# A third buffer for the expert weights' chunks, their product moved later, and VectorE's background work cut smaller

## The chip, the cores and the metric

The kernel runs on one core of a Trainium2 chip, as one launch that covers the whole two-block network. The metric is the device time of one execution in microseconds. Matrix products run on TensorE (PE in the rows; its weight loads are PEld), elementwise work on VectorE (DVE), ScalarE (ACT) and GpSimd (POOL); SyncE (SP) issues most of the loads, ScalarE most of the stores, GpSimd the gathers.

## What is computed

A two-layer block (attention, pooling and convolution branches, then a mixture of 16384 rank-one experts with product keys) is followed by a two-layer conformer block. All is float32. The change touches the expert layer and the start of the next layer's convolution:

```python
def peer_ffn(x, w_q, sub_keys, u_emb, v_emb):          # per 128 tokens, 8 heads, 16 of 16384 experts each
    q = (xc @ w_q).reshape(PEER_CHUNK, PEER_HEADS, 2, PEER_HALF)
    s = jnp.einsum('thid,hikd->thik', q, sub_keys).astype(jnp.float32)
    s1, i1 = lax.top_k(s[:, :, 0], PEER_TOPK)
    s2, i2 = lax.top_k(s[:, :, 1], PEER_TOPK)
    cand = (s1[..., :, None] + s2[..., None, :]).reshape(PEER_CHUNK, PEER_HEADS, PEER_TOPK * PEER_TOPK)
    ...
    gate = jax.nn.softmax(top_s, axis=-1)
    hid = jax.nn.gelu(jnp.einsum('td,thkd->thk', xc, u_emb[eidx]))
    return jnp.einsum('thk,thkd->td', gate * hid, v_emb[eidx])
```

## The kernel before

Every float32 product is made of three matmuls on parts that are split: ScalarE copies a weight tile `raw` into `wh` (rounded to the type that TensorE takes), VectorE or, every few tiles, GpSimd subtracts and leaves `wl` (lines 212 and 223, class `Stream`). `Stream` loads the weight tiles in one fixed order through a ring of five `raw` buffers on SP's queue (line 200); `wl` has a ring of three. `W.pool_every` says which splits GpSimd takes.

The expert layer (`peer`) doesn't gather for its first 384 tokens in layer 0: it multiplies them by all 16384 experts. A **first loop** (128 steps, line 1634 on) makes 128 experts' activations a step from the tile `u`: 24 matmuls of 384 columns, a gelu on ScalarE into `gstage` (ring of three), and a store to `gel` every two steps. Beside it VectorE finds the top keys (`topk_keys`, `route`) and builds from them, with TensorE (line 1531), a dense matrix of gates that goes to `gmat` in twelve stores of 2048 KB. The **second loop** (128 steps, line 1697 on) multiplies by the tile `vv`. Its other operand comes in chunks of four steps: `wload` fetches `gelc` from `gel` and `gmc` from `gmat` (768 KB each) on SP's queue, `wmul` multiplies them on VectorE (line 1604), `wsplit` splits one step's row of the product into `Wh` and `Wl` (ring of four each), two steps ahead of the matmuls (line 1692, 18 of 512 columns a step). Chunks have a ring of two.

The other 128 tokens (`gat`) do gather: 256 times GpSimd fetches a row per token (512 KB in all, `gr`, ring of four, line 1399), and VectorE uses it (lines 1408 and 1423). These run beside both loops; what is left of them is spread over layer 1's convolution and gates (`tail`). Layer 1's modulation is computed by VectorE from raw tiles `modt` (line 516), also in the second loop.

What stands when in each queue is decided as the program is written: `Side` keeps a model of the engines' times. Background work is a generator (`topk_keys`, `route`, `gathered`); each `yield step(...)` is a place at which it may be put off, and `took(engine, ns)` books its cost. `tick` is called between matmuls and runs background steps while neither VectorE nor ScalarE is booked more than `LIM` = 2000 ns ahead. The instructions then stand in that order for good, and every engine works through its own queue in order.

Of the kernel before, what the change touches and what calls it, by code (L numbers as in the profile page):

```python
# [10 lines left out]
F32 = mybir.dt.float32  # L11
F32R = mybir.dt.float32r
# [257 lines left out]
class Side:  # L270
# [8 lines left out]
    def __init__(self, period, ring):  # L279
        self.lanes, self.lates = [], []  # L280
        self.period, self.ring = period, ring
        self.now = self.due = 0.0
        self.slot = [0.0] * 4
        self.free = {"a": 0.0, "v": 0.0, "p": 0.0}
        self.seq = 0
        self.floor = False
        self.rate, self.pe = RATE, 1.0

# [85 lines left out]
    def tick(self, dt):  # L374
        self.now += dt * self.pe
        while True:
            while any(x[0] <= self.now for x in self.lates):
                self._late()
            if self.now < self.due or max(self.free["v"], self.free["a"]) > self.now + LIM:
                return  # L380
            for lane in self.lanes:
                if self._ready(lane[1]) <= self.now:
                    self._run(lane)
                    break
            else:
                return
# [18 lines left out]
def tile_dit_peer_conformer(ctx: ExitStack, tc: tile.TileContext, A, out):  # L405
# [834 lines left out]
    def seg_tail(pool, ns, upd, halves, hs, ss, ab, banks, fill=None, then=None):  # L1240
# [9 lines left out]
        if fill is None:  # L1250
            norm_cols(pool, xs, ab[0], 0, 2 if ns == 2 else 3, banks, then)
            W.pool_every = 0 if ns == 1 else 2
            W.pump(3)
            if ns == 2:
                rest(2)
            return
# [13 lines left out]
    def peer(l, hcp, kp, keys, early):  # L1270
# [14 lines left out]
        with ExitStack() as st:  # L1285
# [37 lines left out]
            def took(eng, ns):  # L1323
                return cur["side"].spend(eng, ns) if sp and cur["side"] else 0.0
# [35 lines left out]
            if sp:  # L1360
                side.rate, side.pe = RATE2, 1.09
            sel = select()
# [65 lines left out]
            def route():  # L1428
                for t in (range(nt) if not sp else (3, 0, 1, 2)):
                    v4 = sv[:, t].rearrange("p (h i) k -> p h i k", i=2)  # L1430
                    cand = tk.tile([128, 8, 16, 16], F32, name="cand", bufs=1)
                    if sp:
                        yield step()
                    for h in range(8):
                        (nc.vector if sp else nc.gpsimd).tensor_add(cand[:, h], v4[:, h, 0, :, None].to_broadcast([128, 16, 16]),
                                                                    v4[:, h, 1, None, :].to_broadcast([128, 16, 16]))
                    took("v", 3000)
                    ts = tk.tile([128, 8, 16], F32, name="ts", bufs=2)
# [20 lines left out]
                    for i in range(2):  # L1459
                        for h0 in (0, 4):  # L1460
                            hh = slice(h0, h0 + 4)
                            eq = tk.tile([128, 4, 16, 16], F32, name="eq", bufs=1)
                            nc.vector.tensor_tensor(eq, abf[:, i, hh, :, None].to_broadcast([128, 4, 16, 16]),
                                                    iota16[:, None, None, :].to_broadcast([128, 4, 16, 16]), op=OP.is_equal)
                            nc.vector.tensor_mul(eq, eq, sif[:, hh, i, None, :].to_broadcast([128, 4, 16, 16]))
                            nc.vector.tensor_reduce(IN[:, t, i].rearrange("p (h k) -> p h k", h=8)[:, hh], eq, axis=AX.X, op=OP.add)
                            took("v", 3700)
                            yield step(TKW * 1.3)
# [86 lines left out]
                for q in range(0, TD // 4, 2):  # L1555
                    if sp:
# [4 lines left out]
                    nc.vector.tensor_tensor(Am, iotac[:, None, :].to_broadcast([128, 8, 128]),  # L1561
                                            IT[:, 1, q * 4:q * 4 + 8, None].to_broadcast([128, 8, 128]), op=OP.is_equal)
                    nc.vector.tensor_tensor(Bk, iotas, spread(IT[:, 0], q), op=OP.is_equal)
                    took("v", 1950)
                    if len(pend) > 2:
# [27 lines left out]
            def wload(c):  # L1593
                g = vq.tile([128, CI, TD], F32, name="gelc", bufs=2)
                nc.sync.dma_start(g, gel_d[c])
                m = vq.tile([128, ntb, CI, TB], F32, name="gmc", bufs=2)
                nc.sync.dma_start(m, g_d[:, :, c * CI:(c + 1) * CI, :].rearrange("b p c t -> p b c t"))
                ld[c] = (g, m)
# [12 lines left out]
            def wsplit(i):  # L1611
                c, r = divmod(i, CI)
                g = ld[c][0]
                wh = vp.tile([128, TD], F32R, name="Wh", bufs=4)
                wl = vp.tile([128, TD], F32R, name="Wl", bufs=4)
                split(wh, wl, g[:, r])
# [9 lines left out]
            for i in range(128):  # L1626
# [3 lines left out]
                if i % GB == 0:  # L1630
                    gs = gp.tile([128, GB, TD], F32, name="gstage", bufs=3)
                h, lo = W.next("u", l, i)
# [19 lines left out]
                if i == 118:  # L1652
# [8 lines left out]
                    vq = vq_stack.enter_context(tc.tile_pool(name=f"pw{l}", bufs=2))  # L1661
                    wload(0)
                    wload(1)
                    if l == 0:
# [32 lines left out]
            for i in range(128):  # L1697
                c, r = divmod(i, CI)
                if r == 0 and c + 1 < nch:
                    wmul(c + 1)  # L1700
                if i + 2 < 128:
                    wsplit(i + 2)
                if r == CI - 1 and c + 2 < nch:
                    wload(c + 2)
# [732 lines left out]
```

## Time and profile before

| | us |
|---|---|
| median of 3 runs | 4544.48 (4543.31 to 4550.07) |
| the profiled execution | 4539.79 |
| its span, first to last instruction | 4538.0 |
| layer 0's first expert loop | 816 to 1434 |
| layer 0's second expert loop | 1434 to 2215 |
| layer 1's convolution and gates with the last gathered rows | 2215 to 2400 |
| layer 1's second expert loop | 3142 to 3505 |

All times in the rows are from the span's start. The stages' bounds are where the rows of the lines named above begin and end. A group of instructions is told by its line, its engine and what it writes and reads (`wl<-raw,wh`).

### The profile page before, as it was taken

The numbers are of one execution on the slowest core, as the hardware profiler recorded it, in microseconds if no ns is written. First come the engines' busy times: TensorE is split into PE (matmuls) and PEld (weight loads), VectorE is DVE, ScalarE is ACT, GpSimd is POOL, SyncE is SP. The second block draws the span as 40 slices with busy tenths as digits, with TensorE's granted clock in tenths as the row PEclk, the third lists the DMA queues.
The fourth block names the chain that finished last, engine by engine and source line by source line (L and its number), as shares of the span: only waits on it lengthen the run. The fifth ranks groups of instructions, "written<-read, shape, count | busy, mean of one in ns | idle before, by whom it ended". The sixth has DMA issues, their size and how long they took to land. (4 is left out here: it accounts for less than half of the span.)

```text
span 4538.0 us, 66430 instructions
## 1 busy us (share of the span) xinstructions
PE 4215.3 (93%) x25423; PEld 3735.4 (82%) x25423; DVE 3221.3 (71%) x5177; ACT 1970.2 (43%) x2939; POOL 1128.6 (25%) x871
## 2 busy tenths in 40 slices
PE   8999999999998877777779989999999999999999
PEld 5887878999997666666678879999887998999988
DVE  6747766999996766566786878786666577555855
ACT  4224443334662222222334444575445445444544
POOL 0012343333117412222543446201443000000000
PEclk9999999999999888888899989999999999999999
DMA  6532232456889877878783336778886644556344
GB/s 218 166 99 69 72 101 97 151 194 234 293 293 343 278 259 270 289 276 283 249 301 110 107 124 206 237 282 306 281 280 237 215 154 132 187 181 215 116 160 156
DMA packets 304824, 932.29 MB, mean 205 GB/s; under 512 B 27752, under 2 KB 95736, under 8 KB 299640
## 3 DMA queue, kind: packets, MB, share of 16 engines
q1 hardware_dynamic: 244000, 696.86, 46.1%
q0 software_dynamic: 37040, 135.29, 8.3%
q10 hardware_dynamic: 23464, 95.88, 5.6%
q8 instruction: 199, 3.26, 0.3%
q14 instruction: 121, 0.99, 0.1%
HBM read 841.94 MB, written 85.99 MB: 204 GB/s over the span
## 5 line engine op out<-in xcount | busy, mean ns | idle before, releaser
L212 ACT ACTIVATE wh<-raw 128x1024 fp32r<-128x1024 f32 (+1 forms) x1086 | 1131.4, 1045 | 1093.4 <-DMA raw<-in_vv 516.4
L469 PE MATMUL pA<-xH,wl 128*128 128x256 f32 (+2 forms) x4600 | 1422.0, 309 | 57.3 <-DVE wl L223 46.1
L223 DVE TENSOR_TENSOR wl<-raw,wh 128x1024 fp32r<-128x1024 f32 (+2 forms) x956 | 1185.5, 1249 | 365.2 <-issue 185.5
L467 PE MATMUL pA<-xH,wh 128*128 128x256 f32 (+2 forms) x4600 | 1439.6, 313 | 1.7 <-ACT xH L472 1.3
L468 PE MATMUL pA<-xL,wh 128*128 128x256 f32 (+2 forms) x4600 | 1417.2, 308 | 0.5 <-DVE xL L473 0.3
L469 PEld LDWEIGHTS pA<-xH,wl 128*128 128x128 f32 x4600 | 876.1, 190 | 93.0 <-DVE wl L223 55.4
L467 PEld LDWEIGHTS pA<-xH,wh 128*128 128x128 f32 x4600 | 877.0, 191 | 34.8 <-issue 6.0
L468 PEld LDWEIGHTS pA<-xL,wh 128*128 128x128 f32 x4600 | 877.1, 191 | 26.6 <-DVE xL L473 1.1
L223 POOL TENSOR_TENSOR wl<-raw,wh 128x1024 fp32r<-128x1024 f32 (+1 forms) x130 | 322.8, 2484 | 731.8 <-PE pA L469 362.8
L1692 PE MATMUL pA<-wl,Wh 128*128 128x512 f32 x1024 | 349.9, 424 | 150.4 <-DVE wl L223 150.4
L1692 PEld LDWEIGHTS pA<-wl,Wh 128*128 128x128 f32 x1024 | 203.2, 202 | 211.1 <-DVE wl L223 163.9
L1692 PE MATMUL pA<-wh,Wl 128*128 128x512 f32 x1024 | 344.5, 419 | 1.7 <-DVE Wl L473 1.7
L1692 PE MATMUL pA<-wh,Wh 128*128 128x512 f32 x1024 | 335.3, 409 | 6.2 <-ACT Wh L472 6.2
L1399 POOL DMA_INDIRECT gr<-in_ur,gi x128 | 185.8, 1451 | 530.9 <-DVE gr L1408 498.8
L468 PE MATMUL pA<-wl,xH 128*128 128x256 f32 (+2 forms) x800 | 272.1, 340 | 10.2 <-POOL wl L223 6.2
L467 PE MATMUL pA<-wh,xH 128*128 128x256 f32 (+2 forms) x800 | 277.9, 347 | 1.8 <-ACT xH L472 1.8
L469 PE MATMUL pA<-wh,xL 128*128 128x256 f32 (+2 forms) x800 | 271.5, 339 | 1.1 <-DVE xL L473 1.1
L1399 POOL DMA_INDIRECT gr<-in_vr,gi x128 | 176.3, 1377 | 340.1 <-DVE gx L1423 297.7
L1609 POOL TENSOR_TENSOR gelc<-gelc,gmc 128x256 f32<-128x256 f32 x128 | 147.9, 1189 | 422.4 <-DMA gmc<-gmat 398.6
L1692 PEld LDWEIGHTS pA<-wh,Wl 128*128 128x128 f32 x1024 | 206.8, 202 | 54.5 <-DVE Wl L473 2.4
L1692 PEld LDWEIGHTS pA<-wh,Wh 128*128 128x128 f32 x1024 | 200.3, 196 | 56.2 <-ACT Wh L472 6.5
L458 POOL TENSOR_TENSOR segr<-segr,nhalf 128x1 f32<-128x1 f32 (+1 forms) x24 | 13.9, 579 | 886.3 <-DVE segr L547 886.3
(456 smaller groups left out, 6305.4 us busy)
## 6 DMA issues: line engine op xcount, KB each, us to landing
raw<-in_u SPq DMA_DIRECT2D x256, 512.0 KB
raw<-in_vv SPq DMA_DIRECT2D x256, 512.0 KB
raw<-in_modt SPq DMA_DIRECT2D x80, 512.0 KB
gmat<-gst ACTq DMA_DIRECT2D x20, 2048.0 KB
raw<-in_conv SPq DMA_DIRECT2D x48, 512.0 KB
raw<-in_gate SPq DMA_DIRECT2D x48, 512.0 KB
gel<-gstage ACTq DMA_DIRECT2D x64, 384.0 KB
gelc<-gel SPq DMA_DIRECT2D x32, 768.0 KB
```

The lines of the kernel that those rows point to most:

```text
L212: self.nc.scalar.activation(h[:, :w], t[:, :w], AF.Copy)
L223: e.tensor_sub(lo[:, :w], t[:, :w], h[:, :w].bitcast(F32))
L458: nc.gpsimd.tensor_tensor(r, r, nhalf[:, 0:1].to_broadcast([128, w]), op=OP.pow)
L467: nc.tensor.matmul(o, s[0], m[0], start=start, stop=False)
L468: nc.tensor.matmul(o, s[0], m[1], start=False, stop=False)
L469: nc.tensor.matmul(o, s[1], m[0], start=False, stop=stop)
L1399: nc.gpsimd.indirect_dma_start(t, None, tabs[j // 128], bass.IndirectOffsetOnAxis(ap=gi[:, k:k + 1], axis=0))
L1609: nc.gpsimd.tensor_mul(gv, gv, m[:, :, ci])
L1692: nc.tensor.matmul(acc[t][dh], s_, m_[:, dh * 512:(dh + 1) * 512], start=(i == 0 and n == 0), stop=(i == 127 and n == 2))
```

## The change

In layer 0 (`sp`): `gelc` and `gmc` get three buffers, three chunks are loaded ahead of the second loop, and chunk c+3 is asked for at the third step of chunk c. The product `wmul(c + 1)` moves from a chunk's first step to its third, next to the first split that reads it. `Wh` and `Wl` go from four buffers to three and `gstage` from three to two. For VectorE's background the limit is 1200 ns in place of 2000, the eight sums for `cand` are booked one by one with a place to put off after four, the three instructions of each `eq` chain get such places between them, and two bookings are adjusted. The tail of layer 0 leaves `W.pool_every` at 0, so GpSimd takes no split in layer 1's first conv tiles.

```diff
@@ class Side @@
-        self.rate, self.pe = RATE, 1.0
+        self.rate, self.pe, self.lim = RATE, 1.0, LIM
-            if self.now < self.due or max(self.free["v"], self.free["a"]) > self.now + LIM:
+            if self.now < self.due or self.free["v"] > self.now + self.lim or self.free["a"] > self.now + LIM:
@@ seg_tail @@
-            W.pool_every = 0 if ns == 1 else 2
+            W.pool_every = 0
@@ peer @@
-                side.rate, side.pe = RATE2, 1.09
+                side.rate, side.pe, side.lim = RATE2, 1.09, 1200
@@ route @@
                     for h in range(8):
+                        if sp and h == 4:
+                            yield step()
                         (nc.vector if sp else nc.gpsimd).tensor_add(cand[:, h], ...
-                    took("v", 3000)
+                        took("v", 380)
...
                             nc.vector.tensor_tensor(eq, abf[:, i, hh, :, None].to_broadcast([128, 4, 16, 16]),
+                            took("v", 1250)
+                            if sp:
+                                yield step()
                             nc.vector.tensor_mul(eq, eq, sif[:, hh, i, None, :].to_broadcast([128, 4, 16, 16]))
+                            took("v", 1250)
+                            if sp:
+                                yield step()
                             nc.vector.tensor_reduce(IN[:, t, i].rearrange("p (h k) -> p h k", h=8)[:, hh], eq, axis=AX.X, op=OP.add)
-                            took("v", 3700)
+                            took("v", 1250)
@@ wload, wsplit, the loops @@
-                g = vq.tile([128, CI, TD], F32, name="gelc", bufs=2)
+                g = vq.tile([128, CI, TD], F32, name="gelc", bufs=3 if sp else 2)
-                m = vq.tile([128, ntb, CI, TB], F32, name="gmc", bufs=2)
+                m = vq.tile([128, ntb, CI, TB], F32, name="gmc", bufs=3 if sp else 2)
-                wh = vp.tile([128, TD], F32R, name="Wh", bufs=4)
-                wl = vp.tile([128, TD], F32R, name="Wl", bufs=4)
+                wh = vp.tile([128, TD], F32R, name="Wh", bufs=3 if sp else 4)
+                wl = vp.tile([128, TD], F32R, name="Wl", bufs=3 if sp else 4)
-                    gs = gp.tile([128, GB, TD], F32, name="gstage", bufs=3)
+                    gs = gp.tile([128, GB, TD], F32, name="gstage", bufs=2 if sp else 3)
-                    wload(0)
-                    wload(1)
+                    for c in range(3 if sp else 2):
+                        wload(c)
-                if r == 0 and c + 1 < nch:
+                if r == (CI - 2 if sp else 0) and c + 1 < nch:
                     wmul(c + 1)
                 if i + 2 < 128:
                     wsplit(i + 2)
-                if r == CI - 1 and c + 2 < nch:
+                if sp and r == CI - 2 and c + 3 < nch:
+                    wload(c + 3)
+                if not sp and r == CI - 1 and c + 2 < nch:
                     wload(c + 2)
```

The first place is the second loop. SP's queue of loads around chunk 11, before (the numbers tell buffers apart; `raw_14392` and `raw_14420` are the tiles of two steps):

```order
L200 DMA raw_14392<-in_vv 128x1024
L200 DMA raw_14420<-in_vv 128x1024
L1595 DMA gelc_14447<-gel0_11_5869 128x1536
L1597 DMA gmc_14449<-gmat0_5890 128x12x128
L200 DMA raw_14455<-in_vv 128x1024
```

VectorE's queue around the product of the same chunk, before:

```order
L1604 TENSOR_TENSOR gelc_14447<-gelc_14447,gmc_14449 128x1536
L473 TENSOR_TENSOR Wl_14485<-gelc_14318,Wh_14484 128x384
L223 TENSOR_TENSOR wl_14492<-raw_14392,wh_14451 128x1024
L473 TENSOR_TENSOR Wl_14515<-gelc_14318,Wh_14514 128x384
L223 TENSOR_TENSOR wl_14520<-raw_14420,wh_14490 128x1024
L1408 SCALAR_TENSOR_TENSOR gr_14378,gz_5918<-gr_14378,gx_5917 128x1024
```

Before, the product stands ahead of the splits of two tiles that SP asks for ahead of the chunk.

SP's queue around chunk 11, now:

```order
L200 DMA raw_14228<-in_vv 128x1024
L1604 DMA gelc_14259<-gel0_11_5869 128x1536
L1606 DMA gmc_14261<-gmat0_5890 128x12x128
L200 DMA raw_14267<-in_vv 128x1024
L200 DMA raw_14296<-in_modt 128x1024
L200 DMA raw_14302<-in_vv 128x1024
L200 DMA raw_14330<-in_vv 128x1024
L200 DMA raw_14359<-in_modt 128x1024
L200 DMA raw_14365<-in_vv 128x1024
L1604 DMA gelc_14390<-gel0_12_5870 128x1536
L1606 DMA gmc_14392<-gmat0_5890 128x12x128
L200 DMA raw_14398<-in_vv 128x1024
```

VectorE's queue around its product, now:

```order
L223 TENSOR_TENSOR wl_14490<-raw_14398,wh_14460 128x1024
L1408 SCALAR_TENSOR_TENSOR gr_14288,gz_5918<-gr_14288,gx_5917 128x1024
L1408 SCALAR_TENSOR_TENSOR gr_14351,gz_5918<-gr_14351,gx_5917 128x1024
L516 SCALAR_TENSOR_TENSOR sjunk_5907,modc1_98<-raw_14359,S_5906 128x1024 x2
L522 TENSOR_TENSOR modc1_98<-modc1_98,pcol_88 128x16
L1613 TENSOR_TENSOR gelc_14259<-gelc_14259,gmc_14261 128x1536
L473 TENSOR_TENSOR Wl_14523<-gelc_14259,Wh_14522 128x384
```

Now seven raw tiles, the last of them `raw_14398`, are asked for after the chunk and used ahead of its product, and the product stands right before the first split that reads it.

The second place is GpSimd's queue at the start of layer 1's convolution, before (the first row's gathers are those of the second loop):

```order
L1399 DMA gr<-in_vr,gi 128x1024 x4
L223 TENSOR_TENSOR wl<-raw,wh 128x1024
L1399 DMA gr<-in_vr,gi 128x1024 x3
L223 TENSOR_TENSOR wl<-raw,wh 128x1024
L1399 DMA gr<-in_vr,gi 128x1024 x26
```

and now:

```order
L682 TENSOR_TENSOR hc_13072<-hc_13072,tmpo 128x512 x2
L720 MEMSET upad_17515 128x272
L720 MEMSET upad_17516 128x272
L1399 DMA gr<-in_vr,gi 128x1024 x48
```

Five splits (two of them in the rows) left GpSimd's queue for VectorE's, and 65 gathers are issued here where 52 were.

## Rows read from the trace of the kernel before

**Rows 1.** The page's first part: each engine's busy us, share of the span, instructions.

```profile
PE 4215.3 (93%) x25423; PEld 3735.4 (82%) x25423; DVE 3221.3 (71%) x5177; ACT 1970.2 (43%) x2939; POOL 1128.6 (25%) x871
```

**Rows 2.** Windows: us, busy PE PEld DVE ACT POOL, clock, DMA share, GB/s.

```profile
880.00:1060.00 180.00, 168.31 (x935) 165.56 (x933) 175.04 (x313) 66.82 (x87) 66.29 (x31) 0.98 0.52 184
1060.00:1360.00 300.00, 298.10 (x2185) 282.83 (x2185) 278.79 (x361) 194.19 (x220) 54.33 (x34) 0.99 0.81 289
1360.00:1434.00 74.00, 63.30 (x343) 61.07 (x343) 45.71 (x65) 23.36 (x34) 48.43 (x54) 0.95 0.99 371
1434.00:2215.00 781.00, 617.63 (x2355) 484.42 (x2353) 512.10 (x641) 199.07 (x279) 242.18 (x203) 0.87 0.79 275
2215.00:2400.00 185.00, 145.28 (x1054) 139.10 (x1055) 155.99 (x174) 61.17 (x90) 92.95 (x69) 0.90 0.77 269
...
3142.00:3505.00 363.00, 360.48 (x1555) 289.62 (x1553) 239.24 (x267) 177.29 (x263) 135.88 (x115) 1.00 0.78 271
```

**Rows 3.** Waits of VectorE and TensorE, 1434 to 2215: us, times, longest.

```profile
DVE gelc L1604 <- DMA gmc<-gmat: 243.9, 29, 10.4
...
PE pA L1692 <- DVE wl L223: 150.4, 31, 7.8
```

**Rows 4.** Timeline around one chunk: start, us, instruction, idle time before it.

```profile
1709.39 1.22 PE L1692 MATMUL pA<-wl,Wh 128*128 128x512 f32 x2 [3.57 <-DVE wl L223]
...
1711.26 1.05 PE L1692 MATMUL pA<-wh,Wh 128*128 128x512 f32 x2
1712.11 1.05 PE L1692 MATMUL pA<-wl,Wh 128*128 128x512 f32 x2
...
1715.65 0.63 PE L1692 MATMUL pA<-wh,Wh 128*128 128x512 f32 x2
1716.11 0.63 PE L1692 MATMUL pA<-wl,Wh 128*128 128x512 f32 x2
...
1716.89 0.44 SPq L1597 DMA_DIRECT2D gmc<-gmat  x1
...
1730.02 1.76 DVE L1604 TENSOR_TENSOR gelc<-gelc,gmc 128x1536 f32<-128x1536 f32 x1 [9.00 <-DMA gmc<-gmat]
```

**Rows 5.** Windows again, three short ones.

```profile
1370.00:1380.00 10.00, 9.46 (x54) 9.14 (x52) 4.44 (x7) 3.48 (x5) 2.34 (x3) 1.00 1.01 409
...
1709.00:1714.00 5.00, 4.61 (x11) 3.65 (x12) 5.00 (x8) 0.95 (x1) 1.68 (x1) 0.50 0.60 165
...
2300.00:2360.00 60.00, 46.94 (x348) 44.82 (x347) 53.88 (x65) 19.90 (x28) 32.36 (x29) 0.91 0.91 334
```

**Rows 6.** DMA's busy share in tenths, 40 slices of 1 us from 1710.

```profile
DMA  6976998998999999999940006916869889999999
```

**Rows 7.** DMA packets of the second loop, 1434 to 2215.

```profile
DMA packets 96852, 214.78 MB, mean 275 GB/s; under 512 B 6064, under 2 KB 52144, under 8 KB 96816
```

**Rows 8.** The page's DMA issues: count and KB each.

```profile
gmat<-gst ACTq DMA_DIRECT2D x20, 2048.0 KB
...
gel<-gstage ACTq DMA_DIRECT2D x64, 384.0 KB
```

**Rows 9.** Waits of the first loop, 816 to 1434.

```profile
ACT gstage L1642 <- PE pA L469: 179.6, 74, 7.4
...
DVE gr L1408 <- DMA gr<-in_ur,gi: 28.2, 14, 6.3
...
PE pA L469 <- DVE wl L223: 22.5, 11, 3.0
```

**Rows 10.** Layer 1's convolution, 2215 to 2400: groups of VectorE and GpSimd, one wait.

```profile
L1423 DVE SCALAR_TENSOR_TENSOR gx<-gr,gz,gx 128x1024 f32<-128x1024 f32 x56 | 76.1, 1359 | 12.8 <-DMA gr<-in_vr,gi 12.0
L223 DVE TENSOR_TENSOR wl<-raw,wh 128x1024 fp32r<-128x1024 f32 x36 | 47.9, 1333 | 0.0
...
L223 POOL TENSOR_TENSOR wl<-raw,wh 128x1024 fp32r<-128x1024 f32 x6 | 15.8, 2628 | 21.2 <-ACT wh L212 21.2
...
PE pA L469 <- POOL wl L223: 9.2, 3, 3.9
```

More of the change, by code (lines that the diff above doesn't have):

```diff
@@ L1562, in route @@
                                             IT[:, 1, q * 4:q * 4 + 8, None].to_broadcast([128, 8, 128]), op=OP.is_equal)
+                    took("v", 1250)
                     nc.vector.tensor_tensor(Bk, iotas, spread(IT[:, 0], q), op=OP.is_equal)
-                    took("v", 1950)
+                    took("v", 700)
                     if len(pend) > 2:
```

## The prediction

> **What bounds the kernel now.** I read the stages first [rows 2], because the shares of the whole span [rows 1] average over stages with different limits: TensorE is busy 93% of it, so a gain can come only from a stage where it is not. The profiled execution took 4539.79 us, its span 4538.0; the median of the timed runs is 4.7 us longer, and I add that at the end. In layer 0's second expert loop (1434 to 2215 us) TensorE is busy 617.63 of 781.00 us at a granted clock of 0.87. In layer 1's second loop, which has neither gathered rows nor the modulation's raw tiles, it is busy 360.48 of 363.00 at 1.00. The first loop of layer 0 loses some 12 us between 880 and 1060 and 11 us at its end. Layer 1's convolution (2215 to 2400) loses 40.
>
> Next the waits of the second loop [rows 3]: VectorE stands 243.9 us, 29 times, in front of the product gelc*gmc for the DMA of gmc. TensorE then waits 150.4 us, 31 times, for VectorE's weight split, which is queued behind that product. One chunk of four steps in time [rows 4]: SP issues the load of gmc at 1716.89; VectorE is through with all else 9.00 us before 1730.02, where the product starts, 13 us after the issue. TensorE waits 3.57 us in the chunk before and then runs pairs of matmuls at 0.85 us where undisturbed ones take 0.466; the clock's row for that place is 0.50 [rows 5], the lower of its two levels.
>
> Last the sixteen DMA engines (below: the link) in the same stretch [rows 6]: sixteen slices in a row at 0.8 and more, then one at 0.4 and three at nothing. The link is full while the late chunk is carried and idle while everybody catches up. Its mean share is 0.79 at 275 GB/s [rows 2], so the chunk's wait is only half latency: behind it stands a link that is not far from full.
>
> **Part 1: three chunk buffers, a late product.** On SP a chunk's loads now stand seven raw tiles ahead of the one whose split is next to the product; before, the product stood ahead even of a split whose tile had been asked for earlier than the chunk. Seven tiles are five steps and two of the modulation's: 30 us at the loop's pace of 781/128 = 6.1 us a step, and still 21 us at TensorE's best of 4.2 (below), against the 13 us of [rows 4]. So the wait for gmc goes. What is late next?
>
> TensorE alone: 128 steps x 18 matmuls x 0.233 us [rows 4] = 537 us. VectorE alone: 512 us busy [rows 2], less three gathered rows (counted on VectorE's order: 133 in this loop before, 130 now) = 508 us. The link: 214.78 MB were moved [rows 7], 212 without those rows (0.52 MB each) and without one chunk (1.57 MB) that is now loaded ahead. 275/0.79 = 348 GB/s is what a full link carries with this mix of packets (half of them under 2 KB), so 212 MB need 608 us. **The link is the longest, so the loop becomes link-bound**, at the share it can hold. Neighbouring stretches where much was queued hold 0.99 (1360 to 1434) and 0.91 (2300 to 2360) [rows 2, 5]; 0.89 is my lower end. That gives 614 to 683 us; I take 0.95, between the two rows since SP still issues in order behind VectorE's splits: 640 us, **141 us less** (98 to 167).
>
> Its costs. The third chunk is loaded before the loop, where the link is already full (0.99): 1.57 MB/0.371 = 4 us there, taken back in the loop (it is in the 212 MB). Wh and Wl with three buffers in place of four: the wl ring beside them has three already, and VectorE waits there for the same TensorE step as Wl would, so the wait moves half a microsecond forward: nothing. The gstage ring of two: a store must land in three steps and not five, and three steps are 3 x 618/128 = 14 us; it is 384 KB behind at most one store of 2048 KB [rows 8], 2.5 MB at 0.289 = 8.6 us. ScalarE's gelu waits 179.6 us for TensorE [rows 9], and no wait of it for a store is listed. Nothing, 12 times 1 us at worst.
>
> **Part 2: VectorE's background in smaller steps** (first loop). TensorE waits there 22.5 us for VectorE's splits [rows 9]. The work itself is unchanged and VectorE is 97% busy between 880 and 1060 (175.04 of 180), so smaller lumps only place it better. On the order the longest run of background between two splits falls by under 1 us (an eq chain of three instructions is cut only now and then). I take -4 us, from -15 to 0.
>
> **Part 3: gathered rows move back.** The tighter limit lets 10 fewer rows into the first loop (57, was 67), three fewer into the second, and 69 instead of 56 into layer 1's convolution and gates. There both are dense: VectorE 155.99 of 185, the link 0.77, and 0.91 in its middle [rows 2, 5]. By VectorE 13 rows cost 13 x 1.36 = 17.7 us [rows 10], by the link 13 x 0.52/0.334 = 20 us; idle time there (29 us of VectorE) may take up to half.
>
> **Part 4: no GpSimd splits in the first conv tiles.** Five splits of 2.63 us leave GpSimd and cost VectorE 5 x 1.33 = 6.7 us; TensorE's three waits for GpSimd's splits, 9.2 us, go [rows 10], and gathers are issued earlier. Parts 3 and 4 together: 10 + 6.7 to 20 + 6.7, less up to 9.2: +14 us, range +5 to +24.
>
> **The sum.** 4539.8 - 141 - 4 + 14 = 4409; with 4.7 for the median, **4413 us**. Its own range: 4539.8-167-15+5+4.7 = 4368 to 4539.8-98+24+4.7 = 4470.
>
> **The rivals.**
> (B) *The link gives more and TensorE bounds.* Between 1370 and 1380 us it carried 409 GB/s at 1.01 [rows 5]; 212 MB would need 518 us, under TensorE's 537. Then 537 + 10 for the start = 547: -234 - 4 + 14 gives 4320. Against it: that stretch holds large packets, while half of this loop's are under 2 KB [rows 7]. The Trainium skill (DMA: Bandwidth & Descriptors, Specifications) gives 435 GB/s as the fabric's ceiling and about 358 as a core's share of the HBM. By the first 212 MB would take 487 us, which is this rival; by the second 592, which is my forecast's side; the trace's 348 at a full link agrees with the second.
> (C) *Short waits remain and keep the clock low.* A link-bound loop still has a wait in most chunks, and after the wait in [rows 4] six pairs ran at 0.85 instead of 0.466, 2.5 us. Then a chunk costs 16.8 + 2.5 + the 2.2 us by which the link is late = 21.5 us, 32 of them 688: -93 - 4 + 18 gives 4465. For it: the clock is at 0.87 over this loop [rows 2]. Against: TensorE has 2.2 us a chunk to spare if waits are shorter than 3.57 us. The Trainium skill (TensorE: Matmul & The Clock Gate, HAM oscillation) says that a loop that waits for a DMA at every tile starts every tile at the low clock; this trace agrees for the waits of [rows 4], and shows 0.98 and 0.99 from 880 to 1360, where no wait is over 3.0 us [rows 2, 9].
> (D) *Slower: the wait changes its name.* With the link full, VectorE could wait for gathered rows or raw tiles as it now waits for gmc, for instance behind four gather buffers that are no deeper than before. If all 243.9 us come back, the loop stays at 781 and the convolution pays 13 rows and five splits in full: 20 + 6.7 gives 4571. It decides once the loop gains under 27 us, that is if the link's share stays below 608/754 = 0.81. For it: in the first loop VectorE waits 28.2 us for gathered rows [rows 9], with the link at 0.81 and, at its end, 0.99 [rows 2]. Against it: TensorE is busy 63.30 of 74.00 us in just that end, which is 0.86 and not the 0.79 of this loop.
> (E) *The chunk wait stays*, because SP's issue of the loads is itself held by a split: 4535 to 4553. Against it: the order has the loads seven tiles earlier.
>
> **How the numbers follow.** Forecast 0.60, C 0.20, B 0.12, D 0.05, E 0.03. The prediction is the forecast's 4413. The range 4350 to 4485 holds the forecast's own range and C with some room for it, and leaves out B, D and E (0.20). Within 0.2% (about 9 us, what a measurement of this kernel can tell from no change) lies E: 0.03; faster 0.92, slower 0.05.
>
> **What would show it.** In the second loop: VectorE's wait for gmc under 30 us; the link's share 0.92 or more; 615 to 680 us; ScalarE's wait for raw tiles (DMA) as what ends last. A share under 0.85 with waits for gathered rows speaks for D; a clock below 0.9 with a share near 0.88 for C; TensorE busy over 97% for B. In the first loop ScalarE's gelu must not wait for a DMA. In layer 1's convolution: 69 gathered rows, 5 to 24 us more, no split of GpSimd among TensorE's waits. It would be wrong altogether if the loop's bytes were not the 212 MB counted here, or if a full link carried this mix at another rate than 348 GB/s.

## The result and the profile after

The changed kernel takes 4361.73 us (median of 4 runs, 4359.04 to 4364.86) against 4543.9 beside it: ratio 0.9602, interval 0.9582 to 0.9622. In five more runs it took 4363.14, ratio 0.9612 (0.9599 to 0.9625). The forecast was 4413. The profiled execution took 4364.86 us. The page's first part, to be read against [rows 1]: TensorE's busy time has fallen by 56 us and the span by 175, so its share has risen.

```profile
PE 4158.8 (95%) x25423; PEld 3692.2 (85%) x25423; DVE 3223.1 (74%) x5180; ACT 1968.2 (45%) x2939; POOL 1123.1 (26%) x868
```

The stages are cut at two lines. The second loop of layer 0 runs from the first start of its matmuls (line 1692 before, 1701 after) to the last start of its `pB<-wl,Wh`; the convolution and gates of layer 1 end with the last start of L784. The view of one line of the kernel before (instructions, ns min/median/max, first and last start):

```profile
L1692 PE MATMUL pA<-wh,Wh x1024: 388/396/796, 1444.1 to 3501.6; 128*128 128x512 f32 x171
L1692 PE MATMUL pB<-wl,Wh x256: 389/396/632, 1452.1 to 2212.0; 128*128 128x512 f32 x128
...
L784 DVE SCALAR_TENSOR_TENSOR merged<-sig,pA x16: 409/548/689, 202.0 to 2391.6; 128x512 f32<-128x512 f32 x8, 128x256 f32<-128x256 f32 x8
```

and of the changed one:

```profile
L1701 PE MATMUL pA<-wh,Wh x1024: 388/396/691, 1440.2 to 3330.6; 128*128 128x512 f32 x171
...
L1701 PE MATMUL pB<-wl,Wh x256: 390/396/628, 1444.9 to 2022.1; 128*128 128x512 f32 x128
...
L784 DVE SCALAR_TENSOR_TENSOR merged<-sig,pA x16: 413/552/689, 204.1 to 2222.8; 128x512 f32<-128x512 f32 x8, 128x256 f32<-128x256 f32 x8
```

So the first loop ends 3.9 us earlier (1440.2 for 1444.1), the second loop takes 581.9 us instead of 767.9 (**-186.0**; forecast -141), convolution and gates 200.7 instead of 179.6 (**+21.1**; forecast +14), and the rest 2140.3 instead of 2146.4. Windows of the changed kernel, columns as in [rows 2]:

```profile
880.00:1060.00 180.00, 174.00 (x975) 172.21 (x974) 174.66 (x350) 68.64 (x90) 62.81 (x31) 0.99 0.54 187
1060.00:1360.00 300.00, 293.60 (x2152) 277.85 (x2150) 275.15 (x345) 190.72 (x217) 43.94 (x28) 0.99 0.77 275
1360.00:1440.00 80.00, 67.71 (x370) 65.27 (x369) 48.41 (x68) 24.64 (x36) 52.72 (x59) 0.96 1.00 371
1440.00:2022.00 582.00, 555.29 (x2318) 436.17 (x2319) 503.75 (x642) 195.74 (x275) 248.41 (x193) 0.98 0.99 360
2022.00:2223.00 201.00, 143.72 (x1002) 137.39 (x1000) 169.48 (x193) 61.58 (x91) 90.62 (x77) 0.87 0.79 276
```

In the second loop both the link (0.99) and TensorE (555 of 582 us, 95%, clock 0.98) are nearly full, where neither was in [rows 2]. Which of them sets the time isn't to be read from this row. Its waits, 1440 to 2022 (engine, line, releaser: us, times, longest), against [rows 3]:

```profile
PE pA L1701 <- DVE wl L223: 16.4, 16, 4.1
PE pA L1701 <- ACT Wh L472: 5.8, 7, 2.0
...
DVE Wl L473 <- ACT Wh L472: 63.9, 49, 4.4
...
ACT wh L212 <- DMA raw<-in_vv: 218.2, 64, 9.7
ACT Wh L472 <- DVE gelc L1613: 119.2, 29, 12.2
```

VectorE no longer waits for gmc at all, and TensorE's wait for its splits has gone from 150.4 us to 16.4. Two loads and two products in time, to set beside [rows 4]:

```profile
1687.74 0.67 SPq L1606 DMA_DIRECT2D gmc<-gmat  x1
...
1705.04 0.43 SPq L1606 DMA_DIRECT2D gmc<-gmat  x1
...
1705.18 1.75 DVE L1613 TENSOR_TENSOR gelc<-gelc,gmc 128x1536 f32<-128x1536 f32 x1
...
1725.05 1.75 DVE L1613 TENSOR_TENSOR gelc<-gelc,gmc 128x1536 f32<-128x1536 f32 x1
...
1725.87 0.63 PE L1701 MATMUL pB<-wh,Wl 128*128 128x512 f32 x2
1727.54 0.73 PE L1701 MATMUL pA<-wh,Wh 128*128 128x512 f32 x2 [1.04 <-ACT Wh L472]
1729.27 0.74 PE L1701 MATMUL pA<-wl,Wh 128*128 128x512 f32 x2 [0.99 <-DVE wl L223]
1729.85 0.63 PE L1701 MATMUL pA<-wh,Wl 128*128 128x512 f32 x2
1730.31 0.63 PE L1701 MATMUL pA<-wh,Wh 128*128 128x512 f32 x2
```

The product now runs without any idle time before it, 20 us apart. By the order of the queues in "The change" (seven raw tiles between a chunk's loads and its product) the product at 1725.05 reads the load issued at 1687.74, 37 us before it; the load of 1705.04 is for the product after it. The product still delays the next splits, but TensorE loses 1.04 and 0.99 us there and, after a first pair at 0.58, goes on at 0.46 us a pair, where before it lost 3.57 and then ran pairs at 0.85.

### The profile page after: what moved, and what is told of

Its sections match the earlier page's. It is cut to its first block, busy times and chain, and to the rows that moved or that the text cites. A ratio compares the mean times of both kernels' runs of the same rounds, so it can differ in the third digit from the quotient of the medians.

```text
span 4363.1 us, 66320 instructions
## 1 busy us (share of the span) xinstructions
PE 4158.8 (95%) x25423; PEld 3692.2 (85%) x25423; DVE 3223.1 (74%) x5180; ACT 1968.2 (45%) x2939; POOL 1123.1 (26%) x868
## 5 line engine op out<-in xcount | busy, mean ns | idle before, releaser
L212 ACT ACTIVATE wh<-raw 128x1024 fp32r<-128x1024 f32 (+1 forms) x1086 | 1130.8, 1044 | 784.8 <-DMA raw<-in_vv 218.2
L223 DVE TENSOR_TENSOR wl<-raw,wh 128x1024 fp32r<-128x1024 f32 (+1 forms) x959 | 1182.6, 1242 | 362.5 <-issue 181.6
L223 POOL TENSOR_TENSOR wl<-raw,wh 128x1024 fp32r<-128x1024 f32 (+1 forms) x127 | 313.2, 2466 | 719.9 <-PE pA L469 348.4
L1701 PE MATMUL pA<-wl,Wh 128*128 128x512 f32 x1024 | 326.8, 400 | 16.7 <-DVE wl L223 16.4
L1701 PE MATMUL pA<-wh,Wh 128*128 128x512 f32 x1024 | 324.5, 397 | 5.9 <-ACT Wh L472 5.8
L1701 PE MATMUL pA<-wh,Wl 128*128 128x512 f32 x1024 | 324.1, 397 | 1.0 <-DVE Wl L473 1.0
L1701 PEld LDWEIGHTS pA<-wl,Wh 128*128 128x128 f32 x1024 | 190.9, 188 | 72.4 <-DVE wl L223 27.6
L473 DVE TENSOR_TENSOR Wl<-gelc,Wh 128x384 fp32r<-128x384 f32 (+1 forms) x256 | 138.3, 541 | 135.9 <-ACT Wh L472 132.7
```

Source lines behind the costliest of these rows:

```text
L212: self.nc.scalar.activation(h[:, :w], t[:, :w], AF.Copy)
L223: e.tensor_sub(lo[:, :w], t[:, :w], h[:, :w].bitcast(F32))
L473: nc.vector.tensor_sub(lo, src, h.bitcast(F32))
L1701: nc.tensor.matmul(acc[t][dh], s_, m_[:, dh * 512:(dh + 1) * 512], start=(i == 0 and n == 0), stop=(i == 127 and n == 2))
```

## The experiments

All stage lengths below are taken as above, from the first and last starts in each kernel's profiled execution (us). Rows are the gathered rows in the first loop, the second loop, and the convolution. "Late" is the product at the last step but one of the chunk before.

| kernel | rows | second loop starts | second loop | conv and gates | rest | time | ratio to before (interval) |
|---|---|---|---|---|---|---|---|
| before | 67/133/56 | 1444.1 | 767.9 | 179.6 | 2146.4 | 4543.9 | 1 |
| changed | 57/130/69 | 1440.2 | 581.9 | 200.7 | 2140.3 | 4361.7 | 0.9602 (0.9582 to 0.9622) |
| changed, again | 57/130/69 | 1438.3 | 580.6 | 198.1 | 2145.7 | 4363.1 | 0.9612 (0.9599 to 0.9625) |
| part 1 alone | 67/133/56 | 1442.3 | 585.8 | 176.7 | 2143.9 | 4351.5 | 0.9599 (0.9583 to 0.9615) |
| smaller steps and limit alone | 57/130/69 | 1438.0 | 768.4 | 201.5 | 2142.3 | 4550.4 | 1.0024 (1.0014 to 1.0034) |
| changed, limit 2000 | 65/132/59 | 1445.4 | 585.4 | 183.7 | 2149.0 | 4366.3 | 0.9622 (0.9606 to 0.9638) |
| part 1 and part 4 | 67/133/56 | 1444.4 | 589.8 | 171.5 | 2144.2 | 4350.6 | 0.9587 (0.9571 to 0.9603) |
| part 1 and part 4, again | 67/133/56 | 1437.8 | 583.2 | 172.5 | 2143.1 | 4352.8 | 0.9595 (0.9581 to 0.9610) |
| late product alone | 67/133/56 | 1438.8 | 595.3 | 179.5 | 2141.4 | 4353.6 | 0.9593 (0.9579 to 0.9607) |
| limit 2600 with parts 1 and 4 | 73/133/50 | 1438.1 | 582.2 | 159.3 | 2146.1 | 4327.5 | 0.9542 (0.9527 to 0.9557) |
| two buffers, late | 57/130/69 | 1437.1 | 582.2 | 201.7 | 2144.6 | 4367.4 | one run |
| three buffers, early | 57/130/69 | 1437.7 | 581.8 | 199.5 | 2142.6 | 4363.4 | one run |
| fewer matmuls | 57/130/69 | 1434.5 | 576.1 | 203.4 | 2147.9 | 4363.6 | one run |
| fewer gathers | 57/130/69 | 1429.5 | 555.1 | 180.8 | 2139.5 | 4306.7 | one run |

The ratio is to runs of the kernel before on the same chip (medians 4533 to 4544); it is worked out from all runs, so it can differ from the quotient of two medians by 0.001. "Rest" is what follows the gates. It holds the same instructions in all of them, and still runs from 2139.5 to 2149.0; differences of under 10 us between two totals say little, and the stages are the better witness.

**What sets the second loop?** My theory was the link, the rival TensorE. One run takes transfers away, one takes matmuls away.

```diff
-                    if j < 256:
+                    if j < 256 and j % 2 and ga["n"] >= 0:
+                        rows[j] = (ga["t"], side.free["v"] + GLAT)
+                    elif j < 256:
-                        t = gat.tile([128, D], F32, name="gr", bufs=NG)
+                        t = ga["t"] = gat.tile([128, D], F32, name="gr", bufs=NG)
```

> The changed kernel with half of the gathered rows left out: every second row reuses the tile that the row before it fetched, so that part of the retrieval is wrong; everything else is computed. VectorE, ScalarE and TensorE have the same instructions; in the second loop some 34 of its 209 MB are gone. Theory (the link sets the loop's 582 us, its engines being busy for .98 of it): 175 MB at the 358 GB/s of the loop are 490 us, so the link is no longer last, and the loop falls to what TensorE needs: 540 to 562 us (537 in the matmuls' own time at the granted clock, 558 as its busy time stands in the loop). The link's share falls to .85 or less. Rival (TensorE with its short waits for VectorE sets the loop): it stays at 576 to 586 us with the link's share at .85.

Its windows, second loop and convolution:

```profile
1429.00:1985.00 556.00, 547.06 (x2320) 437.88 (x2321) 506.50 (x643) 199.30 (x275) 155.68 (x128) 0.99 0.91 315
1985.00:2166.00 181.00, 139.44 (x1003) 133.02 (x1002) 168.93 (x192) 61.46 (x91) 68.03 (x44) 0.91 0.64 211
```

The loop falls from 581.9 to 555.1, with TensorE busy for 547.06 of 556.00. So with 34 MB less it is TensorE that is last, and in the changed kernel it was not. Most of the 27 us are lost late in the loop, as two windows of the changed kernel and one with fewer gathers (the third) show:

```profile
1460.00:1640.00 180.00, 176.68 (x740) 139.26 (x739) 161.63 (x223) 61.52 (x85) 84.86 (x75) 0.99 0.97 349
1680.00:1980.00 300.00, 288.76 (x1207) 226.17 (x1205) 258.29 (x308) 98.84 (x135) 117.50 (x77) 0.99 1.03 383
1680.00:1940.00 260.00, 260.00 (x1116) 208.88 (x1115) 241.39 (x284) 92.55 (x126) 59.06 (x36) 1.00 0.96 339
```

In the first window TensorE is 98% busy beside a link at 0.97, in the second 96% beside 1.03, in the third 100%. (A share above 1 says that the view's share is no exact fraction of the time.) The convolution falls by 20 us with VectorE as busy as before; this is used below.

The other run gives each step of layer 0 12 matmuls of 18:

```diff
-                for n, (s_, m_) in enumerate(((sh, hl[0]), (sh, hl[1]), (sl, hl[0]))):
+                for n, (s_, m_) in enumerate(((sh, hl[0]), (sh, hl[1])) if sp else ((sh, hl[0]), (sh, hl[1]), (sl, hl[0]))):
...
-                                         start=(i == 0 and n == 0), stop=(i == 127 and n == 2))
+                                         start=(i == 0 and n == 0), stop=(i == 127 and n == (1 if sp else 2)))
```

> The changed kernel with a third of the second loop's matmuls left out (12 of 18 in each step: the product with the low part of the chunk's rows), so that layer 0's update is less exact; VectorE, ScalarE and the transfers are the same. TensorE's own time in the loop falls from 537 to some 360 us. Theory (the link sets the loop): 209 MB at 358 to 365 GB/s are 574 to 585 us, so the loop stays at 565 to 590 us, and the wait of the matmuls for VectorE's or ScalarE's splits grows from 29 us to over 150 us. Rival (TensorE sets it): the loop falls to what is next, VectorE's 505 us of busy time: 505 to 530 us. If the time falls between, both held it in turn.

Its second loop, the window and TensorE's waits:

```profile
1434.00:2011.00 577.00, 436.20 (x1552) 314.95 (x1552) 503.60 (x641) 195.50 (x275) 248.59 (x193) 0.89 0.99 363
```

```profile
PE pA L1701 <- DVE wl L223: 81.5, 68, 7.6
PE pA L1701 <- ACT Wh L472: 56.6, 31, 4.1
```

A third of TensorE's work is gone and the loop is 6 us shorter: 576.1. The waits are 138 us, not quite the 150 expected. The link's share stays at 0.99, and VectorE, with 503.60 us, does not bound it either. **The second loop is link-bound**, with TensorE 27 us behind over the whole loop and level with the link in its first part. SP's issue waits as long for VectorE to free a raw buffer in the changed kernel (312.9 us) as with fewer gathers (318.6 us), so these waits don't tell the two loops apart; a deeper ring of raw tiles was not tried.

**Which half of part 1 does it?** Two buffers, late (the load of chunk c+2 where the change loads c+3):

```diff
-                g = vq.tile([128, CI, TD], F32, name="gelc", bufs=3 if sp else 2)
+                g = vq.tile([128, CI, TD], F32, name="gelc", bufs=2)
...
-                m = vq.tile([128, ntb, CI, TB], F32, name="gmc", bufs=3 if sp else 2)
+                m = vq.tile([128, ntb, CI, TB], F32, name="gmc", bufs=2)
...
-                    for c in range(3 if sp else 2):
+                    for c in range(2):
...
-                if sp and r == CI - 2 and c + 3 < nch:
-                    wload(c + 3)
+                if sp and r == CI - 2 and c + 2 < nch:
+                    wload(c + 2)
```

> The changed kernel with two chunk buffers instead of three and the product still late: a chunk's load is issued two steps before the end of the chunk that holds its buffer, and its product is due four steps later, where the kernel before had one step. Theory (it is the lead that counts, and a chunk's 1.5 MB take under three steps of 4.5 us to land): VectorE's wait for a chunk comes back in part only, 0 to 60 us in the loop, which takes 582 to 640 us. Rival (the third buffer is what counts): the buffer is let go only when the last split of its chunk has read it, so that the load lands too late by some 5 us at nearly each of 29 chunks: loop 680 to 740 us.

Three buffers, early:

```diff
-                if r == (CI - 2 if sp else 0) and c + 1 < nch:
+                if r == 0 and c + 1 < nch:
```

> The changed kernel with three chunk buffers, and the product back at the first step of the chunk before. A chunk's load then has six steps until its product is due, instead of eight. Theory (six steps, some 27 us, are enough for 1.5 MB): no wait for a chunk, loop 578 to 592 us, so the late product is worth nothing beside the third buffer. Rival (the early product is queued ahead of the splits at the step where they are wanted, or the load is late in 27 us at a full link): the wait is back by 1 to 3 us at each chunk, loop 610 to 680 us.

Both give the whole gain, 582.2 and 581.8 us, and in neither does VectorE wait for a chunk. So neither the third buffer nor the late product is needed beside the other. The smallest edit is then one line in the kernel before:

```diff
-                if r == 0 and c + 1 < nch:
+                if r == (CI - 2 if sp else 0) and c + 1 < nch:
```

> The kernel before with one edit: the product of a chunk in the second loop stands at the last step but one of the chunk before it instead of the first. Two buffers, the load at the last step, and the rings of four and three stay. A load then has three steps (some 13.6 us) until its product is due, instead of one. Theory (two buffers with a load four steps ahead gave 582 us, so it is the lead alone that counts, and VectorE's wait of 244 us is 29 waits of up to 10 us, less than two steps): the wait falls under 40 us, the loop takes 582 to 610 us, the time is 4350 to 4380. Rival (at a full link a chunk's 1.5 MB beside the other transfers take over three steps to land): a wait of 2 to 4 us is left at most chunks, loop 640 to 700 us, time 4410 to 4470.

Its second loop, the window and VectorE's wait for a chunk:

```profile
1439.00:2034.00 595.00, 562.60 (x2318) 442.60 (x2318) 508.20 (x636) 196.59 (x274) 241.75 (x194) 0.97 0.97 357
```

```profile
DVE gelc L1604 <- DMA gmc<-gmat: 1.8, 4, 0.9
```

Of 243.9 us in 29 waits 1.8 us in 4 are left: the load has three steps instead of one, some 14 us against the 13 of [rows 4]. The loop takes 595.3 us, some 10 more than with part 1, but the time, 4353.6 at a ratio of 0.9593, is that of part 1 alone (4351.5 at 0.9599) within the intervals.

**Parts 1 to 4 apart.** Part 1 alone is the diff's edits of the chunk buffers, the rings, the loads and the product in the kernel before, no more.

> The kernel before with part 1 alone: three chunk buffers, the late product, the rings of three and two; VectorE's steps, the limit of the first loop and GpSimd's splits in layer 1's conv stay as before (67 gathered rows in the first loop, 133 in the second, 56 in the conv). Theory: part 1 alone takes the whole gain of the second loop (768 us before, 582 in the changed kernel), and the 21 us that the conv and its gates lost (179 to 200 us) come from the parts left out here; so loop 580 to 590 us, conv and gates 175 to 185, first loop as before, and a time of 4340 to 4352 us, some 10 to 20 under the changed kernel. Rival: what the conv lost comes from the faster loop itself (it ends before the gathered rows and VectorE's other work are through, or at another clock); then conv and gates take some 195 to 205 us here too and the time is 4360 to 4370. Second rival: part of the loop's gain comes from VectorE's smaller steps; then the loop stays above 600 us and the time is above 4375.

The loop's 585.8 and the convolution's 176.7 us are as the theory said: part 1 has the gain, the rest has the loss. The reverse, all but part 1 and the GpSimd edit:

> The changed kernel with part 1 and the GpSimd edit undone: two chunk buffers, the early product, GpSimd's splits back; what is left is VectorE's work in smaller steps and the lower limit on its queue in the first loop (57 gathered rows there, 130 in the second loop, 69 in the conv). Theory: the second loop's wait for the product stays, so the loop takes 760 to 775 us; the first loop ends 2 to 6 us sooner; the 13 gathered rows more in the conv cost 5 to 21 us; time 4540 to 4562, within half a percent of the kernel before. Rival: the smaller steps let the matmuls' own splits through in the second loop too, and take a part of its 244 us of wait: 4500 or less.

Theory again: 768.4 us in the loop, 201.5 in the convolution (+21.9), and 0.24% slower.

Part 1 with the GpSimd edit (`W.pool_every = 0`):

> The kernel before with part 1 and the GpSimd edit: 67, 133 and 56 gathered rows as before, no split on GpSimd in layer 1's first conv tiles. Against the run with part 1 alone only the five splits differ. Theory: five splits of 1.3 us on VectorE (6.7 us of its time) against 9.2 us of TensorE's wait for GpSimd: conv and gates within 6 us of the run with part 1 alone, time within 6 us of it, so 4338 to 4356. Rival: VectorE is what the conv waits for, and the conv's loss is from here: conv and gates 10 to 20 us longer than with part 1 alone, time 4355 to 4370.

> The kernel before with part 1 and the GpSimd edit, again, on the chip of the changed kernel. Theory (the conv's loss is that of the 13 gathered rows that the lower limit moves there, 6.8 MB that the link must carry there, and the smaller steps bring back 4 us in the first loop alone): 8 to 16 us under the changed kernel, 4346 to 4354 us, conv and gates 170 to 178 us. Rival (the earlier difference of 11 us lay in the two runs): within 4 us of the changed kernel.

The convolution takes 171.5 and 172.5 us, where kernels with GpSimd's splits and 56 rows have 179.6, 176.7 and 179.5: the edit gains some 6 us. VectorE's busy time there did not grow by the 6.7 us of five more splits: it is 153.44 us (window 2034 to 2206) against 155.18 with part 1 alone (2028 to 2205). GpSimd's splits had held VectorE up. In part 1 alone these two rows overlap in time; by itself such a split of VectorE takes 1.22 us:

```profile
2057.59 4.02 DVE L223 TENSOR_TENSOR wl<-raw,wh 128x1024 fp32r<-128x1024 f32 x1
...
2058.16 2.36 POOL L223 TENSOR_TENSOR wl<-raw,wh 128x1024 fp32r<-128x1024 f32 x1
```

The changed kernel beside it, for the small differences:

> The changed kernel as it is, beside the next three on one chip, for differences of under half a percent. Expected: 4358 to 4366 us, ratio 0.960 to 0.962; the second loop at 580 to 584 us and conv and gates at 198 to 203 us.

It is 10.4 us slower than parts 1 and 4 in the medians (4363.1 and 4352.8), though the two intervals (0.9599 to 0.9625, 0.9581 to 0.9610) overlap at their ends. The stages carry it: the convolution's 198.1 against 172.5.

The changed kernel with the old limit:

```diff
-                side.rate, side.pe, side.lim = RATE2, 1.09, 1200
+                side.rate, side.pe, side.lim = RATE2, 1.09, LIM
```

> The changed kernel with the limit on VectorE's queue in the first loop back at its old value (2000 instead of 1200 in the planner's units), everything else as changed: 65 gathered rows in the first loop, 132 in the second, 59 in the conv. Theory: the conv's loss of 21 us goes with its gathered rows (13 more than before): with 3 more it is some 5 us, so conv and gates take 182 to 190 us and the first loop loses the 4 us that it had won or a part of it; time 4346 to 4356, 6 to 16 under the changed kernel. Rival: the loss comes from the splits that VectorE took over from GpSimd, and the rows don't matter: conv and gates stay at 197 to 203 us, and the time is 4360 to 4368.

The convolution's 183.7 us are the theory's; the time is not. The first loop ends 5 us later than in the changed kernel, the second takes 3.5 us more, and the rest, which the edit leaves alone, 9 us more, so that the total came out the same and says nothing on the limit.

**A version that beats both.** The limit goes the other way: up to 2600 in the first loop, where the link is at 0.52 to 0.81 until 1360 us [rows 2], with parts 1 and 4, VectorE's old steps and the two lines of `class Side` that read the limit.

```diff
-                side.rate, side.pe = RATE2, 1.09
+                side.rate, side.pe, side.lim = RATE2, 1.09, 2600
```

> The kernel before with part 1 and the GpSimd edit, and the limit on VectorE's queue in the first loop raised to 2600 (2000 before, 1200 in the changed kernel): 73 gathered rows in the first loop (67), 128 in the second (133), 50 in the conv (56). Theory (a gathered row costs 1.5 us of the link where it is last, and the first loop's link is busy for .77 to .81 only): the second loop 5 to 9 us shorter than with part 1 and the GpSimd edit (2.6 MB at 360 GB/s and up), the conv 4 to 12 us shorter, the first loop 3 to 9 us longer by the matmuls' waits for VectorE there (22.5 us before, 13.7 in the changed kernel); time 4336 to 4350. Rival (VectorE's queue in the first loop costs what the link gains): the first loop ends over 10 us later, time 4350 to 4362.

(The expectation miscounts the second loop's rows: 133, as before, not 128.) Window of its convolution, and L784:

```profile
2020.00:2180.00 160.00, 130.29 (x1003) 125.61 (x1002) 145.58 (x175) 61.49 (x91) 72.64 (x58) 0.95 0.80 285
```

```profile
L784 DVE SCALAR_TENSOR_TENSOR merged<-sig,pA x16: 409/548/687, 202.0 to 2179.6; 128x512 f32<-128x512 f32 x8, 128x256 f32<-128x256 f32 x8
```

4327.5 us, ratio 0.9542: 36 us less than the changed kernel on the same chip, the intervals well apart. The first loop doesn't end later (1438.1), the second loop with its unchanged rows takes as long, and the convolution takes 159.3 us, 13 under that of parts 1 and 4 and 39 under the changed kernel's. The time lies under the 4336 to 4350 that were expected. Against parts 1 and 4 on the same chip it is 25 us in the medians and 11 in the profiled executions, where the stages show the 13 of the convolution; what else the medians hold isn't shown.

## Why the prediction was right, and where its steps failed

**The range.** The time lies in the stated range, 4350 to 4485, but 6 us under the forecast's own (4368 to 4470): the stated one began 18 us lower, for which the prediction gives no reason. That much is luck. The prediction also says that it would be wrong altogether if a full link carried this mix at another rate than 348 GB/s, and it did, as below. The wait that it named did go and the link does bind next; the size of the gain was wrong.

**The chunk wait goes, the link binds: right.** No wait for gmc, and the two runs with less work show the link as what is last. ScalarE's wait for raw tiles is the longest in the list, as forecast, though it fell (515.3 us before, 218.2 now).

**The size of it: the step that failed.** The forecast had 640 us for the window of 781, and the loop's -141 came out as -186, outside the step's own range (98 to 167). With the same ends the changed kernel's window is 1430 to 2025 (its second row: the DMA packets there):

```profile
1430.00:2025.00 595.00, 563.77 (x2365) 443.48 (x2364) 512.65 (x654) 198.58 (x281) 255.56 (x200) 0.98 0.98 358
...
DMA packets 95162, 213.02 MB, mean 358 GB/s; under 512 B 6046, under 2 KB 50590, under 8 KB 95126
```

The bytes were as counted (213.02 for 212 MB). The share is 0.98 and not 0.95: 608/0.98 is 620, 20 us less. And a full link carries 358/0.98 = 365 GB/s, not 348: 212/0.365/0.98 = 593, 27 us less again. The 1 MB more gives 3 back: 596. (Of the 186 us, 54 are TensorE's own: as many matmuls keep it busy for 563.77 us at a clock of 0.98, against 617.63 at 0.87 [rows 2].) The 348 was worked out as 275/0.79, that is, from a link which was not full, on the assumption that bytes and busy share go together. They don't quite. With fewer gathers 315/0.91 is 346; in the changed kernel's later half, shown above, the share reads 1.03 at 383 GB/s, which is 372, and late in the loop of the kernel before 283/0.81 is 349:

```profile
1750.00:2150.00 400.00, 310.71 (x1165) 243.05 (x1163) 249.90 (x288) 95.73 (x131) 103.07 (x74) 0.86 0.81 283
```

Smaller packets are not the reason: from 1460 to 1640 the changed kernel's were 2063 bytes on average (62.85 MB in 30466) at 349/0.97 = 360, from 1460 to 1700 in the kernel before 2130 (64.95 MB in 30496) at 271/0.79 = 343. Why the rate rises isn't shown and stays open. A full link stood in [rows 2], at the end of the first loop: 371/0.99 = 375, and 2300 to 2360 in [rows 5] has 334/0.91 = 367. I used both for the share and not for the loop's rate.

**Rival B** was half right: the link did give more, but it is still last, and TensorE has 95% of the loop, not over 97%. Its limit is known now: 555 us from the first matmul on, with some waits left (forecast 537, and 10 for the start). The Trainium skill (DMA: Bandwidth & Descriptors, Specifications) has about 358 GB/s as a core's share of the HBM. The loop's mean of 358 agrees, the 383 over 300 us does not; the measurement decides, and 358 was no ceiling here. That the prediction's 348 agreed with it rests on the step that failed.

**Rival C** fell: the short waits do remain (16 for VectorE, 7 for ScalarE), but they are 4.1 us at most and mostly near 1, and the clock is at 0.98. The run with fewer matmuls, with 99 waits of 138 us in all and a third less to do, shows 0.89. The Trainium skill (TensorE: Matmul & The Clock Gate, HAM oscillation) tells of a loop whose wait for a DMA is longer than a tile's matmuls and which starts every tile at the low clock; the waits of 1.04 and 0.99 us above, beside some 4.2 us of matmuls a step, are no such case. **D** and **E** fell with the wait for gmc; no other DMA took its place before VectorE (gathered rows 6.4 and 0.5 us).

**The free costs** can't be seen. No wait of ScalarE's gelu for a DMA is listed in the first loop now either. The rings of three and two and the third chunk, taken together, cost nothing that the times show: part 1 alone and the late product alone are 2 us apart. One wait of ScalarE for a raw tile `u` did grow, from 5.7 us at most before to 16.0, but the first loop doesn't end later.

**Part 2, -4 us:** the five profiled executions with the first loop as before start the second loop at 1437.8 to 1444.4 (mean 1441.5), the six with the changed first loop at 1434.5 to 1440.2 (mean 1437.6; fewer gathers left out). That is -3.9, as forecast, but the old limit with the smaller steps gave 1445.4 and the raised limit with the old steps 1438.1, so I don't call the cause shown.

**Parts 3 and 4, +14:** the sum was +21.1, in its range, of two terms that were both off and partly cancelled. Moving the five splits gains some 6 us at 56 rows (at 69 nothing: 201.5 with them on GpSimd, 198.1 to 203.4 without), where I charged a cost of -2.5 to +6.7. The 6.7 us left out that GpSimd's splits hold VectorE up. And 13 rows cost 198.1 to 203.4 less 172.0, that is 26 to 31 us, not 10 to 20; with GpSimd's splits in both kernels they cost 21.9 (201.5 less 179.6). Without GpSimd's splits 50 rows take 159.3, 56 rows 172, 59 rows 183.7, 69 rows 200: 41 us for 19 rows, **2.1 us a row** (between neighbours 2.1, 3.9 and 1.6, and the last two have VectorE's smaller steps as well, so no more than a mean). I had priced a row once by VectorE (1.36 us) and once by the link (1.5 us) and let idle time take up half. VectorE's group for a row in the convolution of the changed kernel, of parts 1 and 4, and with fewer gathers:

```profile
L1423 DVE SCALAR_TENSOR_TENSOR gx<-gr,gz,gx 128x1024 f32<-128x1024 f32 x69 | 90.5, 1312 | 20.1 <-DMA gr<-in_vr,gi 17.8 <-issue 1.6
L1423 DVE SCALAR_TENSOR_TENSOR gx<-gr,gz,gx 128x1024 f32<-128x1024 f32 x56 | 73.7, 1316 | 7.9 <-DMA gr<-in_vr,gi 7.2
L1425 DVE SCALAR_TENSOR_TENSOR gx<-gr,gz,gx 128x1024 f32<-128x1024 f32 x69 | 91.3, 1323 | 1.2
```

and TensorE's wait for VectorE's splits there, in the kernel before (2212 to 2392) and the changed one:

```profile
PE pA L469 <- DVE wl L223: 25.7, 18, 5.3
...
PE pA L469 <- DVE wl L223: 51.0, 21, 5.7
```

A row costs VectorE its 1.3 us and, on top, a wait for its fetch. From 56 to 69 rows the first grows by 16.8 us and the idle time before the rows by 12.2, together the 29 us between the two convolutions (200.7 and 171.5). The run with fewer gathers bears this out: all 69 rows are computed, half of the fetches are gone, VectorE no longer waits for a row, and the convolution is 20 us shorter (180.8), about as much as the 18.9 us by which that idle time fell. So some 17 of the 29 us are VectorE's own work and some 12 its waits for the fetches; the idle time in the stage took up nothing.

The total was 51 us too high: 45 from the loop, 6 from the rest of the program, 8 from the allowance for the median (the profiled execution was 3 us above its median, not 5 below), less 7 in the convolution.

## What to carry to other kernels

Count the steps between a load's issue and the instruction that needs it before adding a buffer: here one line, three steps of lead for one, gave the time that three buffers gave, though its loop was some 10 us longer. When a wait goes, work out the next bound from a stretch of the trace where that resource is really full, not by dividing a part-loaded rate by its share. And background work that a planner pushes out of a stage has a price where it lands; the kernel got faster by letting more of it into the stage whose link had room. Work that is moved between VectorE and GpSimd has to be priced on both, since here one held the other up.

## What was not expected of the hardware

In the second loop the DMA engines moved 339 to 353 GB/s per unit of busy share at shares of 0.79 to 0.96 (the kernel before, fewer gathers), and 360 to 372 at 0.97 to 1.03. The share alone doesn't decide it: in other stages, with other transfers, 289/0.81 is 357 and 334/0.91 is 367 [rows 2, 5]. One core took 383 GB/s for 300 us. A gathered row in a dense stretch cost 2.1 us on average, more than VectorE's 1.3 us or the link's 1.5 us alone. A split of VectorE beside one of GpSimd took 4.02 us instead of 1.22.
